# The second layer's output projection: its last quarter of rows multiplied in plain fp32 instead of as three rounded products

## The chip, the core and the metric

The kernel runs on one core of a Trainium2 chip. The metric is the device time of one execution in microseconds (us). The engines are TensorE (PE, with its weight loads listed apart as PEld), VectorE (DVE), ScalarE (ACT), GpSimd (POOL) and SyncE (SP); here SP only issues the transfers from device memory, in order, and an issue waits on its queue until the buffer it writes is free.

## What is computed

A two-layer decoder trunk over 256 positions of width 2048, all in fp32. The change concerns the last line of the second layer's token mixer, `o @ w_o`, a product of 256x2048 by 2048x2048.

```python
def swa_attention(h, pos, w_in, sinks, w_o):      # layer 1: window 128, 32 heads of 64
    ...
    o = jnp.einsum('bnhgqk,bnkhd->bnqhgd', p, vb).reshape(B, S, Hq * dh)
    return o @ w_o

for i in range(DEPTH):                            # DEPTH = 2
    ...
    h = x * (1.0 + sc1) + sh1
    y = fox_attention(...) if i == 0 else swa_attention(...)
    x = layer_norm(DEEPNORM_ALPHA * x + (1.0 + g1) * y, ...)
    h = x * (1.0 + sc2) + sh2
    y = conv_ffn(h, ...)
    x = layer_norm(DEEPNORM_ALPHA * x + (1.0 + g2) * y, ...)
```

## The kernel before

**Three products for one.** Weights arrive as fp32. `stream` loads them in tiles `w` of 128 partitions x 4 row blocks x 512 columns (1 MB), six buffers in rotation (pool `wp`, shared with the tiles `wa` of the conditioning matrix and `ln` of the norm rows). Two row blocks at a time are split: ACT copies them to `wh` in fp32r, a rounded format that TensorE takes in one go (L255), and DVE puts the rest, `w - wh`, into `wl` (L259). `wh` and `wl` have four buffers each. The other operand is split in the same way, and TensorE adds the products high x high, high x low and low x high in PSUM (`x_mm`).

**Whole products.** A row block `kc` that `stream` finds in `whole` isn't split: it calls `add(kc, w, None, use)`, and `x_mm` then issues one fp32 product of `w` as loaded with an unsplit stationary tile. Before the change layer 0 does this for kc 4-7 and 12-15, layer 1 for none. `o_tile` decides the same for the attention's result `o`: an unsplit one is one ACT copy into a tile `oW` (L784); a split one is an ACT cast (L84) and a DVE subtraction (L85) into `oT`, or, for kc 12-15, into the free rows of the large tile `hH`.

```python
        if kc in WHOLE[l]:
            ...
            nc.scalar.copy(o, src)
            return o, None
...
                if l is None:
                    mm(ps[t], xh, h[:, i, :], start=kc + i == first, stop=kc + i == last)
                    continue
                mm(ps[t], xh, h[:, i, :], start=kc + i == first)
                mm(ps[t], xh, l[:, i, :])
                mm(ps[t], xl, h[:, i, :], stop=kc + i == last)
```

**The projection's course.** `out_proj` makes four column blocks d = 0 to 3 of 512, each for two blocks t = 0, 1 of 128 positions, over 16 row blocks kc: 128 products by 128x512, each threefold in layer 1. Row block kc is the result of two heads. For d = 0 and 1 the kc run in the order 0-7, 8-11, 12-15, between the attention of the last heads (scores `S`, softmax `pr`, transposes `T` and their copies `pT`, results `o`), since `stat` steps the attention on until the result it needs is there. d = 2 and d = 3 follow without attention between.

**The edge.** In the last block, d = 3, `x_mm_end` does kc 8-15 for t = 0 first and then for t = 1. While t = 1 runs, `Edge.end` has DVE finish t = 0: residual (L658, L660), statistics (L662, L665), scaling (L688); then TensorE transposes `x` (`sm`, L539) and ACT and DVE make the next input `hH` (L548 to L552) for the first block of the following ConvFFN, `head_block`. For this block of d = 3 the splits of kc 8 to 15 go to spare places, so that they can be made ahead: kc 8, 10 and 12 into unused room of `hH`, kc 14 into small tiles `eh` and `el`.

**Order.** The instructions of an engine run in a fixed order, chosen by the tile scheduler at build time; buffers that come free decide when a waiting transfer starts.

Of the kernel before, what the change touches and what calls it, by code (L numbers as in the profile page):

```python
# [21 lines left out]
KC = D // P  # L22
# [19 lines left out]
def hybrid_trunk(ctx: ExitStack, tc: tile.TileContext, a: dict, out: bass.AP):  # L42
# [186 lines left out]
    def stream(wsrc, row0, col, ks, use, spare={}, whole=()):  # L229

        ks, pend = list(ks), {}
        for kc in ks[::2]:
            g = row0 + kc
            src = wsrc[g // UK, col // WB]
            if kc in pend:
                w = pend[kc]
            elif g % UK == 0 and kc + 2 in ks:
                W = wtile()
                pin(nc.sync.dma_start(W, src), False)
                w, pend[kc + 2] = W[:, :2], W[:, 2:]  # L240
            else:
                if halves:
                    w = halves.pop()
                else:
                    W = wtile()
                    w = W[:, :2]
                    halves.append(W[:, 2:])
                pin(nc.sync.dma_start(w, src[:, g % UK:g % UK + 2]), False)
            if kc in whole:
                add(kc, w, None, use)  # L250
                continue
            h, l = spare[kc]() if kc in spare else (hl.tile([P, 2, WB], F32R, tag=n, name=n) for n in ("wh", "wl"))
            pieces = [(h, l, w)] if not isinstance(h, Pair) else [(h[:, i, :], l[:, i, :], w[:, i, :]) for i in range(2)]
            for hp, _, wp_ in pieces:
                pin(nc.scalar.copy(hp, wp_), False)  # L255

            def split_(pieces=pieces):
                for hp, lp, wp_ in pieces:
                    nc.vector.tensor_tensor(lp, wp_, f32(hp), op=ALU.subtract)  # L259

            add(kc, h, l, use, split_)
# [22 lines left out]
    def x_mm(ps, kc, h, l, stat, last, first=0, ts=range(NT), js=range(2)):  # L284

        for t in ts:
            for i in js:
                xh, xl = stat(kc + i, t)
# [7 lines that stand above are left out]
    def x_mm_end(ps, stat, nk, n, edge=None):  # L296

        kept = []

        def use(kc, h, l):  # L300
            end = kc >= nk - 2 * n
            x_mm(ps, kc, h, l, stat, nk - 1, ts=(0,) if end else range(NT))
            if end:
                kept.append((kc, h, l))
            if kc + 2 >= nk:
                for i, e in enumerate(kept):
                    if edge:
                        edge(i, ps)
                    x_mm(ps, *e, stat, nk - 1, ts=(1,))
                if edge:  # L310
                    edge(n, ps)

        return use
# [46 lines left out]
    def spares(nk, n, held=False):  # L360
        at = lambda o: hpad[:, o:o + 2 * WB].rearrange("p (a f) -> p a f", a=2)
        if n == 8:
            return {nk - 16 + 2 * i: lambda i=i: (at(32 + i * 4 * WB), at(32 + (2 * i + 1) * 2 * WB)) for i in range(4)}
        out = {nk - 8 + 2 * i: lambda i=i: (at(32 + i * 2 * WB), at(60 + (8 + 2 * i) * WB)) for i in range(4)}
        if held:
            out[nk - 2] = lambda: (Pair("eh"), Pair("el"))
        return out
# [402 lines left out]

    AV = ((0, 0, 2 * P), (P, 2 * P, 3 * P))

    WHOLE = ((*range(4, 8), *range(12, KC)), ())

    wide = []

    def o_tile(kc, src, l):

        if kc in WHOLE[l]:
            if not wide:  # L780
# [13 lines left out]
    def out_proj(oT, full, w_o, l, edge):  # L794
# [7 lines left out]
        def part(d, ks):  # L802
            if d == D // WB - 1:
                stream(w_o, 0, d * WB, ks, x_mm_end(ps[d], stat, KC, HEAD, edge.end), spares(KC, HEAD, True), WHOLE[l])
            else:
                stream(w_o, 0, d * WB, ks, lambda kc, h, l_: x_mm(ps[d], kc, h, l_, stat, KC - 1), whole=WHOLE[l])

# [487 lines left out]
```

## Time and profile before

| | |
|---|---|
| median of 3 runs | 2180.22 us (2179.78 to 2181.76) |
| the profiled execution | 2180.01 us, of which 2178.1 us are the span from the first to the last instruction |
| granted TensorE clock | 0.997 |
| busy | PE 98%, PEld 88%, DVE 80%, ACT 53%, POOL 1% |
| transfers | 598.60 MB, 275 GB/s in the mean |
| layer 1's output projection, kc 12-15 and the edge | about 1380 to 1455 us of the span |

In the rows shown below, a timeline row is the start in us, the duration in us from the first start to the last end, engine, line, operation, output<-inputs, shape and how many instructions are merged in it; in brackets stands idle time of the engine just before it and what ended it. In a row of a group, after the bar, stand busy us and mean ns of one, then idle us before such instructions and what ended it. Matmuls overlap in the pipeline, so the rate of a stretch is read from start to start and not from the durations. The chain is the work that ended last, followed back from the end. Line 75 is the helper that issues every product; a product is told by its tiles.

### The profile page before, as it was taken

The page shows a single profiled execution, that of the slowest core. Times are in us where ns is not written, and L with a number is a line of the kernel's source. Part 1 is how long each engine was busy: PE and PEld are TensorE (multiplying, and loading weights), DVE is VectorE, ACT ScalarE, POOL GpSimd, SP SyncE. Part 2 cuts the span into 40 slices and gives each one's busy share as a digit, 9 for nine tenths or more (in the row PEclk, how much of TensorE's full clock was granted, in tenths as well). Part 3 has the DMA queues.
Part 4 walks back from the last instruction along what each step waited for, and adds up shares of the span by engine and source line. Part 5 has one row for each costly group of instructions (what it writes and reads, how often), then busy time and mean ns, then how long its engine had stood idle before and what let it go on. Part 6 is the DMA issues. An engine that isn't in the chain of part 4 may idle for free.

```text
span 2178.1 us, 35629 instructions
## 1 busy us (share of the span) xinstructions
PE 2133.7 (98%) x14424; PEld 1916.9 (88%) x14424; DVE 1742.4 (80%) x2400; ACT 1151.8 (53%) x1788; POOL 11.8 (1%) x34
## 2 busy tenths in 40 slices
PE   6999999999999999999999999999999999999997
PEld 6999887579999888999987877779999888999986
DVE  7988898779989988988997897679788655666765
ACT  4546565255575433555555577555555633555541
POOL 1000000000000000000000000000000000000000
PEclk9999999999999999999999999999999999999999
DMA  9998988949888989887885665547777555555552
GB/s 389 420 370 305 372 333 333 370 173 352 312 298 316 341 346 356 328 325 291 327 332 224 239 251 195 183 144 299 271 271 272 198 194 195 194 194 194 192 195 100
DMA packets 89654, 598.60 MB, mean 275 GB/s; under 512 B 10016, under 2 KB 12352, under 8 KB 21136
## 3 DMA queue, kind: packets, MB, share of 16 engines
q1 hardware_dynamic: 89312, 595.87, 73.9%
q8 instruction: 113, 1.85, 0.3%
q0 software_dynamic: 176, 0.44, 0.1%
q14 instruction: 53, 0.43, 0.0%
HBM read 594.18 MB, written 2.10 MB: 274 GB/s over the span
## 4 chain that ended last, share of the span: by engine, by line
PE 84%; DVE 9%; ACT 4%; DMA 2%; issue 1%; SPq 0%; POOL 0%; DVEq 0%; ACTq 0%; POOLq 0%
PE ws L75 46%; PE xs L75 35%; DVE wa L420 3%; DVE wl L259 2%; DMA w<-in_fox_w_in_dram 2%; ACT wh L255 1%; DVE pr L735 1%; PE o L75 1%; PE S L75 1%; ACT pr L739 0%; PE T L766 0%; ACT hH L551 0%; PE sm L75 0%; PE sm L502 0%; DVE hH L552 0%
## 5 line engine op out<-in xcount | busy, mean ns | idle before, releaser
L255 ACT CAST wh<-w 128x1024 fp32r<-128x1024 f32 x698 | 733.0, 1053 | 726.8 <-PE ws L75 340.2
L259 DVE TENSOR_TENSOR wl<-w,wh 128x1024 fp32r<-128x1024 f32 x698 | 847.8, 1221 | 328.6 <-ACT wh L255 326.1
L75 PE MATMUL ws<-hH,wh 128*128 128x256 f32 x6400 | 1098.0, 276 | 8.3 <-ACT hH L529 7.5
L75 PEld LDWEIGHTS ws<-hH,wh 128*128 128x128 f32 x6400 | 968.3, 188 | 11.7 <-ACT hH L529 7.9
L75 PE MATMUL ws<-hH,wl 128*128 128x256 f32 x3200 | 879.9, 276 | 2.4 <-DVE wl L259 2.4
L75 PEld LDWEIGHTS ws<-hH,wl 128*128 128x128 f32 x3200 | 601.2, 188 | 3.4 <-DVE wl L259 3.3
L420 DVE CUSTOM_DVE_ANT_0 wa<-wa,cb,acol 128x2048 f32<-128x2048 f32 x192 | 449.4, 2344 | 2.1 <-DMA wa<-in_ada_w_dram 1.9
L75 PE MATMUL xs<-wh,gT 128*128 128x512 f32 x1344 | 414.7, 389 | 0.0
L75 PEld LDWEIGHTS xs<-wh,gT 128*128 128x128 f32 x1344 | 252.3, 188 | 52.1
L75 PE MATMUL xs<-wl,gT 128*128 128x512 f32 x672 | 261.4, 389 | 0.0
L75 PE MATMUL xs<-wh,hH 128*128 128x512 f32 x752 | 254.0, 403 | 6.5 <-ACT wh L255 3.2
L75 PEld LDWEIGHTS xs<-wh,hH 128*128 128x128 f32 x752 | 140.3, 189 | 40.3 <-ACT wh L255 3.7
L75 PE MATMUL xs<-wl,hH 128*128 128x512 f32 x376 | 148.9, 396 | 2.5 <-DVE wl L259 2.5
L75 PEld LDWEIGHTS xs<-wl,gT 128*128 128x128 f32 x672 | 126.1, 188 | 26.3
L1150 ACT ACTIVATE u<-ws,ccol 128x256 f32<-128x256 f32 x176 | 96.7, 561 | 52.3 <-PE ws L75 42.1
L75 PE MATMUL xs<-wh,oT 128*128 128x512 f32 x288 | 96.1, 401 | 1.1 <-ACT wh L255 1.1
L1151 DVE SCALAR_TENSOR_TENSOR u<-ws,ccol,u 128x255 f32<-128x255 f32 x176 | 82.1, 476 | 14.4 <-ACT u L1150 14.4
L75 PEld LDWEIGHTS xs<-wl,hH 128*128 128x128 f32 x376 | 71.0, 189 | 16.9 <-DVE wl L259 3.2
L1153 DVE SCALAR_TENSOR_TENSOR u<-ws,ccol,u 128x254 f32<-128x254 f32 x176 | 83.1, 476 | 2.2
L75 PEld LDWEIGHTS xs<-wh,oT 128*128 128x128 f32 x288 | 53.9, 188 | 13.2 <-ACT wh L255 1.3
L739 ACT ACTIVATE pr<-pr,nm 128x128 f32<-128x128 f32 x96 | 43.2, 452 | 32.0 <-DVE nm L735 31.9
L658 DVE TENSOR_TENSOR t<-xs,gate 128x512 f32<-128x512 f32 x48 | 31.5, 683 | 35.0 <-PE xs L75 35.0
(213 smaller groups left out, 1268.6 us busy)
## 6 DMA issues: line engine op xcount, KB each, us to landing
wa<-in_ada_w_dram SPq DMA_DIRECT2D x192, 1024.0 KB, 6.7
w<-in_ffn_w_up_dram SPq DMA_DIRECT2D x176, 1024.0 KB, 5.3
w<-in_ffn_w_down_dram SPq DMA_DIRECT2D x88, 1024.0 KB, 5.0
w<-in_fox_w_in_dram SPq DMA_DIRECT2D x60, 512.0 KB, 8.7
w<-in_swa_w_in_dram SPq DMA_DIRECT2D x20, 1024.0 KB, 5.7
w<-in_fox_w_in_dram SPq DMA_DIRECT2D x18, 1024.0 KB, 7.5
w<-in_fox_w_o_dram SPq DMA_DIRECT2D x16, 1024.0 KB, 7.3
w<-in_swa_w_o_dram SPq DMA_DIRECT2D x16, 1024.0 KB, 4.8
```

The costliest lines, as they stand in the source:

```text
L75: return nc.tensor.matmul(o, lhsT, rhs, start=start, stop=stop, **kw)
L255: pin(nc.scalar.copy(hp, wp_), False)
L259: nc.vector.tensor_tensor(lp, wp_, f32(hp), op=ALU.subtract)
L420: return nc.vector.tensor_tensor_reduce(w, w, cb, 1.0, acol[:, l, v * KC + k:v * KC + k + 1], ALU.mult, ALU.add, cv[:, k:k + 1])
L658: pin(nc.vector.tensor_tensor(tmp, ps[t], gate[:, d * 512:(d + 1) * 512], op=ALU.mult), end)
L735: nc.vector.tensor_tensor_reduce(pr[:, b:e].rearrange("p (a k) -> p a k", k=P), S_ps[:, b:e].rearrange("p (a k) -> p a k", k=P), mk, -1.0, ...
L739: nc.scalar.activation(pr[:, b:e], pr[:, b:e], AF.Exp, bias=nm[:, r:r + 1], scale=-1.0, accum_out=ss[:, r:r + 1])
L1150: nc.scalar.activation(u, pf, AF.Identity, bias=cw(CW, f), scale=cw(2, f))
L1151: nc.vector.scalar_tensor_tensor(u[:, 1:], pf[:, :S - 1], cw(1, f), u[:, 1:], op0=ALU.mult, op1=ALU.add)
L1153: nc.vector.scalar_tensor_tensor(u[:, 2:], pf[:, :S - 2], cw(0, f), u[:, 2:], op0=ALU.mult, op1=ALU.add)
```

## The change

In layer 1 the row blocks kc 12-15 are no longer split: neither the weights (for all four d) nor the attention's results.

```diff
-    WHOLE = ((*range(4, 8), *range(12, KC)), ())
+    WHOLE = ((*range(4, 8), *range(12, KC)), range(12, KC))
```

32 products (4 kc x 4 d x 2 t) of three instructions become 32 of one. Eight splits of weights go (six of the `wh`/`wl` pairs, one in `hH`, one in `eh`/`el`), and four splits of `o` become copies. It also moves instructions. On TensorE, at the last heads' attention, the stretch of kc 12-15 began so before, in d = 0 (`T` transposes softmax rows, `o` is an attention result, and the `hH` here holds the split `o` of kc 12-15):

```order
L766 MATMUL T<-ident,pr 128x128 x3
L75 MATMUL xs<-wh,hH 128x512
L75 MATMUL xs<-wl,hH 128x512
...
L75 MATMUL xs<-wh,hH 128x512
L75 MATMUL o<-pT,V 64x256 x2
L75 MATMUL o<-pT,V 64x128 x2
L766 MATMUL T<-ident,pr 128x128 x6
L75 MATMUL xs<-wh,hH 128x512
L75 MATMUL xs<-wl,hH 128x512
L75 MATMUL o<-pT,V 64x256 x2
L75 MATMUL o<-pT,V 64x128 x2
```

And begins so now, on the same engine at the same place, to the end of d = 1:

```order
L766 MATMUL T<-ident,pr 128x128 x3
L75 MATMUL xs<-w,oW 128x512 x4
L75 MATMUL o<-pT,V 64x256 x2
L75 MATMUL o<-pT,V 64x128 x2
L766 MATMUL T<-ident,pr 128x128 x4
L75 MATMUL xs<-w,oW 128x512
L766 MATMUL T<-ident,pr 128x128 x2
L75 MATMUL o<-pT,V 64x256
L75 MATMUL xs<-w,oW 128x512
L75 MATMUL o<-pT,V 64x256
L75 MATMUL o<-pT,V 64x128 x2
L75 MATMUL xs<-w,oW 128x512 x10
```

The attention's steps keep their order, and the whole products stand between them singly: one splits the six transposes, one the last `o`.

On TensorE at the edge (d = 3, the end of t = 1, with the transposes `sm` of the new `x`), the difference from before (-) to now (+):

```order
-L75 MATMUL xs<-hH 128x512 x3
+L75 MATMUL xs<-w,oW 128x512
 L539 MATMUL sm<-ident,x 128x128 x4
-L75 MATMUL xs<-hH 128x512 x3
+L75 MATMUL xs<-w,oW 128x512
 L539 MATMUL sm<-ident,x 128x128 x4
-L75 MATMUL xs<-eh,hH 128x512
-L75 MATMUL xs<-el,hH 128x512
-L75 MATMUL xs<-eh,hH 128x512 x2
-L75 MATMUL xs<-el,hH 128x512
-L75 MATMUL xs<-eh,hH 128x512
+L75 MATMUL xs<-w,oW 128x512 x2
```

The transposes stay where they were; one whole product stands ahead of them, one between the two groups and two behind, where three, three and six rounded ones were.

On SP's queue the transfers keep their order, and what they wait for changes. The last two tiles of this projection's weights and the first of the next ones stood so before (a `DMAHW` wait is for an earlier transfer, the other one for the engine that frees the buffer):

```order
L239 DMA w<-in_swa_w_o_dram 128x2048 [waits DMAHW1_49,DVE_49]
L239 DMA w<-in_swa_w_o_dram 128x2048 [waits DMAHW2_49,DVE_49]
L239 DMA w<-in_ffn_w_up_dram 128x2048 [waits DMAHW3_49,DVE_49]
...
L239 DMA w<-in_ffn_w_up_dram 128x2048 [waits DMAHW5_49,DVE_49]
L239 DMA w<-in_ffn_w_up_dram 128x2048 [waits DMAHW6_49,DVE_49]
L239 DMA w<-in_ffn_w_up_dram 128x2048 [waits DMAHW1_49,DVE_49]
L239 DMA w<-in_ffn_w_up_dram 128x2048 [waits DMAHW2_49,DVE_49]
```

And so now:

```order
L239 DMA w<-in_swa_w_o_dram 128x2048 [waits DMAHW7_49,PE_49]
L239 DMA w<-in_swa_w_o_dram 128x2048 [waits DMAHW0_49,PE_49]
L239 DMA w<-in_ffn_w_up_dram 128x2048 [waits DMAHW7_49,DVE_49]
...
L239 DMA w<-in_ffn_w_up_dram 128x2048 [waits PE_49]
L239 DMA w<-in_ffn_w_up_dram 128x2048 [waits DMAHW1_49,DVE_49]
L239 DMA w<-in_ffn_w_up_dram 128x2048 [waits DMAHW2_49,DVE_49]
L239 DMA w<-in_ffn_w_up_dram 128x2048 [waits DMAHW0_49,PE_49]
```

A tile read as loaded is freed by TensorE's last product with it, no longer by DVE's subtraction: the four transfers that wait for PE are those that take such a tile's buffer. On ACT the casts of d = 3's kc 8 and 10 now stand ahead of the last ten of the `wh`.

## Prediction

> **What bounds the kernel now.** I read first the busy times and the chain of the page, then TensorE's waits around the place of the change, 1340 to 1480 us.
>
> ```profile
> span 2178.1 us, 35629 instructions
> PE 2133.7 (98%) x14424; PEld 1916.9 (88%) x14424; DVE 1742.4 (80%) x2400; ACT 1151.8 (53%) x1788; POOL 11.8 (1%) x34
> PE 84%; DVE 9%; ACT 4%; DMA 2%; issue 1%; SPq 0%; POOL 0%; DVEq 0%; ACTq 0%; POOLq 0%
> PE S L75 <- DVE qL L85: 0.8, 1, 0.8
> PE xs L75 <- ACT hH L84: 0.7, 1, 0.7
> PE sm L539 <- DVE x L688: 0.6, 1, 0.6
> ```
>
> TensorE is busy 98% of the span and holds 84% of the chain. In these 140 us it waits three times, 2.1 us in all, and never for a split of weights. So time is made or lost here by the TensorE time of the products, except at the edge, where 0.6 and 0.7 us say that DVE and ACT end last. The splits themselves are early, as the ACT and DVE groups of 1352 to 1440 us show:
>
> ```profile
> L255 ACT CAST wh<-w 128x1024 fp32r<-128x1024 f32 x24 | 25.2, 1048 | 21.0 <-PE xs L75 20.7
> L84 ACT CAST hH<-o 128x256 fp32r<-128x256 f32 x4 | 1.5, 368 | 1.0 <-PE o L75 1.0
> L259 DVE TENSOR_TENSOR wl<-w,wh 128x1024 fp32r<-128x1024 f32 x25 | 30.5, 1222 | 20.7 <-ACT wh L255 20.6
> L85 DVE TENSOR_TENSOR hH<-o,hH 128x256 fp32r<-128x256 f32 x4 | 1.7, 419 | 0.9 <-ACT hH L84 0.9
> ```
>
> ACT sat idle 20.7 us before its casts until TensorE gave a `wh` back: it waits for TensorE, not the other way round.
>
> **What is removed costs nothing and brings nothing.** Off ACT go eight casts of 1.05 us, 8.4 in all. Off DVE go eight subtractions of 1.22 and four of 0.42: 11.4 us. (One cast and one subtraction of the eight are made in halves, for `eh` and `el`; I price them as whole.) All this lay beside TensorE's stream. The four copies of `o` stay at about 0.37 us. What could be won by it is at most the 1.3 us of waits at the edge; since there DVE and ACT run the norm and no split of this projection, I take 0 and keep -1.3 as the lower end.
>
> **The price of a product.** Layer 0 has the same whole products, with the same shapes.
>
> ```profile
> L75 PE MATMUL xs<-w,oW 128*128 128x512 f32 x128 | 57.0, 593 | 0.0
> 377.52 3.60 PE L75 MATMUL xs<-w,oW 128*128 128x512 f32 x8
> 380.96 0.82 PE L75 MATMUL o<-pT,v 128*128 128x256 f32 x4
> 406.96 7.03 PE L75 MATMUL xs<-w,oW 128*128 128x512 f32 x16
> 1394.74 0.39 PE L75 MATMUL xs<-wh,oT 128*128 128x512 f32 x1
> 1411.06 0.39 PE L75 MATMUL xs<-wh,hH 128*128 128x512 f32 x1
> 1416.50 0.39 PE L75 MATMUL xs<-wh,oT 128*128 128x512 f32 x1
> ```
>
> Layer 0 makes 8 kc x 4 d x 2 t = 64 such products, and the first row counts 128: each leaves two records. Sixteen records from 406.96 take 7.03 to the last one's end; less its own 0.59 that is 6.44 over 15 starts, 0.429 each, and the eight from 377.52 to 380.96 give 0.430. A whole product takes 0.859 us. The rounded ones: d = 2 runs 96 of them from 1394.74 to 1416.50, 0.2267 each, 0.680 for three. A whole product costs 0.179 us more than the three it replaces, and all 32 would cost 5.7 us if nothing hid any of it.
>
> The Trainium skill, TensorE: Matmul & The Clock Gate, section Back-to-back issue gap, gives about 131 ns for a 512-column matmul in a stream with weight loads, and about 216 ns from its formula for an isolated gap. With the four passes that the Trainium skill, FP8 and Floating Point Precision, section TensorE Precision Notes, gives for true fp32, an estimate from these pages is that a product would cost 0.13 us more by the first and 0.22 by the second, 4.2 or 6.9 us over 32. The 0.2267 here agrees with neither, and the rows decide.
>
> **d = 2.** 24 rounded products from 1411.06 to 1416.50, 5.44 us, become 8 whole ones, 6.87: +1.43 on the path.
>
> **d = 0 and 1, among the attention.**
>
> ```profile
> 1380.60 0.49 PE L766 MATMUL T<-ident,pr 128*128 128x128 f32 x3
> 1380.85 0.49 PE L75 MATMUL xs<-wh,hH 128*128 128x512 f32 x1
> 1383.80 0.87 PE L75 MATMUL o<-pT,V 128*64 128x256 f32 x8
> 1384.60 0.88 PE L766 MATMUL T<-ident,pr 128*128 128x128 f32 x6
> 1385.28 0.50 PE L75 MATMUL xs<-wh,hH 128*128 128x512 f32 x1
> 1385.93 1.04 PE L75 MATMUL o<-pT,V 128*64 128x256 f32 x8
> 1386.90 0.73 PE L75 MATMUL xs<-wh,hH 128*128 128x512 f32 x2
> ```
>
> From 1380.60 to 1394.74 pass 14.14 us. `T` and `o` take 0.25, 0.80, 0.68 and 0.97 of it, start to next start; 11.44 are left for 48 rounded products, 0.56 more than 48 x 0.2267, lost at the switches to and from `T` and `o`. Sixteen whole ones take 13.74: +2.30 if these switch losses vanish, as in layer 0, where the eight records ahead of `o` at 380.96 ran at full rate; +2.86 if they stay. New is that two groups are cut up: one whole product follows the first four of the transposes and needs the new copy of `o`, and the last `o` is split around another. The copy, 0.37 us, has the four transposes as cover (about 0.45, two thirds of the 0.68 above); the copies `pT` have whole products of 0.86. I take 0.15 for what isn't covered, so +2.45, between 2.30 and 2.86.
>
> **d = 3 and the edge.**
>
> ```profile
> 1430.15 1.55 PE L75 MATMUL xs<-hH 128*128 128x512 f32 x6
> 1432.92 2.94 PE L75 MATMUL xs<-hH,oT 128*128 128x512 f32 x12
> 1433.12 0.69 DVE L658 TENSOR_TENSOR t<-xs,gate 128x512 f32<-128x512 f32 x1 [3.23 <-PE xs L75]
> 1437.11 0.65 PE L539 MATMUL sm<-ident,x 128*128 128x128 f32 x4 [0.57 <-DVE x L688]
> 1437.52 0.93 PE L75 MATMUL xs<-hH 128*128 128x512 f32 x3
> 1438.29 0.60 PE L539 MATMUL sm<-ident,x 128*128 128x128 f32 x4
> 1438.64 0.48 PE L75 MATMUL xs<-eh,hH 128*128 128x512 f32 x1
> 1440.12 0.39 PE L75 MATMUL xs<-wh,hH 128*128 128x512 f32 x1
> 1440.64 0.68 DVE L658 TENSOR_TENSOR t<-xs,gate 128x512 f32<-128x512 f32 x1
> 1443.17 0.42 DVE L552 TENSOR_TENSOR hH<-t,hH 128x256 fp32r<-128x256 f32 x1
> 1443.64 0.73 PE L75 MATMUL xs<-wh,hH 128*128 128x512 f32 x2
> 1454.58 0.50 PE L75 MATMUL xs<-wh,hH 128*128 128x512 f32 x1 [0.73 <-ACT hH L84]
> ```
>
> For t = 0, the twelve from 1430.15 to 1432.92, 2.77 us, become four whole, 3.44: +0.67 on the path, since DVE starts the norm when they end. For t = 1, four whole ones replace twelve too, but here a cover exists. The transposes at 1437.11 wait for DVE, 4.19 us after t = 0's end; ahead of them one whole product replaces three rounded ones, +0.18, inside the 0.57 of waiting. Behind them three whole ones (2.58) replace the nine of 1437.52 to 1438.29 and 1438.64 to 1440.12 (2.25): t = 1 ends 0.33 later. DVE needs that end for its residual at 1440.64, and as it took 0.20 from 1432.92 to 1433.12, it could have begun at 1440.32; with 0.33 more it begins at 1440.65. DVE stays the later one, by a hair. The next block's products would then reach the place of 1443.64, where they awaited DVE's row of 1443.17, about 0.1 late. I take +0.10, with 0.72 as the upper end (nothing hidden) and 0 as the lower. If this cover goes, the residual of t = 1 is what starts late, and with it the wait shown at 1454.58.
>
> **The transfers.** Four issues on SP wait for TensorE now, and those behind them in its queue wait too.
>
> ```profile
> w<-in_swa_w_o_dram SPq DMA_DIRECT2D x16, 1024.0 KB, 4.8
> 1392.36 0.33 SPq L239 DMA_DIRECT2D w<-in_swa_w_o_dram  x1
> 1429.91 0.33 SPq L239 DMA_DIRECT2D w<-in_ffn_w_up_dram  x1
> 1464.41 1.06 ACT L255 CAST wh<-w 128x1024 fp32r<-128x1024 f32 x1 [1.75 <-PE xs L75]
> ```
>
> The tile with d = 3's kc 8-11, issued at 1392.36, now waits for d = 0's last whole product, about 1391 (1380.60, nine whole products, 2.70 of `T` and `o`), so it lands with the 4.8 of the first row near 1396. Its two casts now stand ahead of those for d = 2's kc 8 on ACT. With two casts of 1.05 before, one for itself and a subtraction of 1.22, that split would be ready near 1400.5; it is needed 48 rounded products, 10.9 us, after d = 2's start near 1397: cover of some 7 us. The last of the four, issued at 1429.91 before, waits for the edge's end near 1445, and its tile is cast at about 1464 + 5: cover some 19 us for a 5 us transfer. Both 0; the price of a miss is in the rivals.
>
> **The sum.** 2.45 + 1.43 + 0.67 + 0.10 = 4.65. On the profiled execution's 2180.01 us (2178.1 of span and 1.9 around it), which stands 0.21 below the median 2180.22, that is 2184.7, a little past the 0.2% (4.4 us, about what a measurement of this kernel tells from no change).
>
> **Rivals.** *Nothing of the edge is hidden, and the switch losses stay*: 2.86 + 1.43 + 0.67 + 0.72 = 5.7, so 2185.7. For it speaks how thin the cover is (0.01 us by the row of 1440.64), against it the 0.57 us of waiting.
>
> *Less than 0.2%*: no switch is lost, t = 1 is hidden whole, and the lighter ACT and DVE shorten the edge's waits by up to 1.3: 2.30 + 1.43 + 0.67 - 1.3 = 3.1, so 2183.1. For it speaks that the edge is DVE's and ACT's; against it, that after 1433 us neither has a split that is removed.
>
> *Faster, the other side*: a whole product costs one record. Its place is each of the 32, its price 0.429 against 0.680, -8.0 us, so 2172.0; it decides if a product issues below 0.680. For it stands that each record, 0.429, is below that; against it the count of 128 for 64 products and the eight records between 377.52 and 380.96, which are one `w` pair's four products (two kc, two t). The Trainium skill, Perfetto Trace Analysis, section Engine Utilization, halves the array's rate for FP32_LOW_HIGH; were that a whole product's rate, it would be this rival, and the trace has 0.859 against 0.2267, about a quarter of the rate.
>
> *A late tile*: d = 2's kc 8 casts starve behind those of `hH`. If the tile landed a whole landing time (4.8) past the cover of 7, TensorE would wait about 5 more: 2189.5. Nothing in the queue's rows speaks for a delay of 12 us.
>
> **Chances.** Forecast 0.58, nothing hidden 0.20, less than 0.2% 0.15, faster 0.03, late tile 0.04. The forecast lies at the threshold, so about half of its 0.58 falls on either side: slower 0.30 + 0.20 + 0.04 = 0.54, same 0.28 + 0.15 = 0.43, faster 0.03. The range reaches over the first two rivals, 2183.1 to 2185.7, with 0.1 below and 0.5 above, since of the shown runs (2179.78 to 2181.76) the median lies nearer the fast end: 2183.0 to 2186.2. Left out are faster, late tile and a tenth of the rest.
>
> **What would show it.** In the trace after: 64 more `w,oW` records at 0.43 from start to start; d = 2 about 1.4 longer than 21.76; 1380.60 to d = 2's start about 16.6 instead of 14.14; the wait for `x` near 0.4 instead of 0.57; from t = 0's end to the place of 1454.58 the same 21.7 us within 0.2. Wrong would it be made by a wait of TensorE at d = 2's kc 8, by a longer edge, or by whole products that run at another rate beside the 64-column `o`.

## The result, and the profile after

The changed kernel takes 2187.36 us, median of 7 runs (2185.91 to 2188.41); the kernel before, run beside it, 2180.07 (2179.41 to 2181.76). The ratio is 1.0032 with a 95% interval of 1.0023 to 1.0041: slower by 7.3 us, where the prediction had 4.65, and outside its range of 2183.0 to 2186.2. The profiled execution of the changed kernel is the one at 2187.36, with a granted clock of 0.997 as before.

The head of its page, the chain by engine, and TensorE's waits from 1340 to 1480 us, as shown of before:

```profile
span 2185.4 us, 35534 instructions
PE 2139.9 (98%) x14392; PEld 1911.2 (87%) x14392; DVE 1732.9 (79%) x2387; ACT 1144.2 (52%) x1779; POOL 11.8 (1%) x34
PE 84%; DVE 9%; ACT 4%; issue 1%; DMA 1%; SPq 0%; POOL 0%; DVEq 0%; ACTq 0%; POOLq 0%
PE S L75 <- DVE qL L85: 0.8, 1, 0.8
PE xs L75 <- ACT hH L84: 0.7, 1, 0.7
PE sm L539 <- DVE x L688: 0.4, 1, 0.4
```

TensorE is busy 6.2 us longer (2139.9 against 2133.7), DVE 9.5 and ACT 7.6 us less (the prediction had 11.4 and 8.4), and the waits around the change are the three of before, 1.9 us in all instead of 2.1. The view lists no new wait (it leaves out those under 0.15 us): the time went into TensorE's own work. The groups of the changed kernel by line and tiles:

```profile
L75 PE MATMUL xs<-w,oW 128*128 128x512 f32 x192 | 86.2, 594 | 0.0
L259 DVE TENSOR_TENSOR wl<-w,wh 128x1024 fp32r<-128x1024 f32 x692 | 840.9, 1221 | 332.2 <-ACT wh L255 329.8
L255 ACT CAST wh<-w 128x1024 fp32r<-128x1024 f32 x692 | 726.6, 1053 | 730.2 <-PE ws L75 339.7
```

The 64 more records of whole products are there, 192 instead of 128, and six `wh`/`wl` pairs fewer.

To see where the 7.3 us lie, the run is cut at four places that both traces have: the last copy `qb` of layer 1's queries (before the change takes effect), the three transposes `T` ahead of kc 12-15, the first `wl,oT` product of d = 2 and of d = 3, and the edge, the product that waits for `hH`. TensorE's rows of the changed kernel from `T` to d = 2, those of rounded products left out:

```profile
1380.88 0.49 PE L766 MATMUL T<-ident,pr 128*128 128x128 f32 x3
1381.21 3.60 PE L75 MATMUL xs<-w,oW 128*128 128x512 f32 x8
1384.74 0.87 PE L75 MATMUL o<-pT,V 128*64 128x256 f32 x8
1385.54 0.66 PE L766 MATMUL T<-ident,pr 128*128 128x128 f32 x4
1386.08 1.12 PE L75 MATMUL xs<-w,oW 128*128 128x512 f32 x2
1387.04 0.38 PE L766 MATMUL T<-ident,pr 128*128 128x128 f32 x2
1387.35 0.65 PE L75 MATMUL o<-pT,V 128*64 128x256 f32 x2
1387.93 1.12 PE L75 MATMUL xs<-w,oW 128*128 128x512 f32 x2
1388.98 0.86 PE L75 MATMUL o<-pT,V 128*64 128x256 f32 x6
1389.78 8.85 PE L75 MATMUL xs<-w,oW 128*128 128x512 f32 x20
1398.70 0.39 PE L75 MATMUL xs<-wl,oT 128*128 128x512 f32 x1
```

and its later landmarks, TensorE's first `wl,oT` of d = 3 and the edge, with DVE's two residuals:

```profile
1421.93 0.40 PE L75 MATMUL xs<-wl,oT 128*128 128x512 f32 x1
1439.00 0.69 DVE L658 TENSOR_TENSOR t<-xs,gate 128x512 f32<-128x512 f32 x1 [3.90 <-PE xs L75]
1446.70 0.69 DVE L658 TENSOR_TENSOR t<-xs,gate 128x512 f32<-128x512 f32 x1 [0.38 <-PE xs L75]
1460.66 0.50 PE L75 MATMUL xs<-wh,hH 128*128 128x512 f32 x1 [0.73 <-ACT hH L84]
```

The same two `wl,oT` rows of the kernel before:

```profile
1394.96 0.39 PE L75 MATMUL xs<-wl,oT 128*128 128x512 f32 x1
1416.72 0.39 PE L75 MATMUL xs<-wl,oT 128*128 128x512 f32 x1
```

`wl,oT`, the second product, is taken because a first rounded product that follows a whole one has a longer record (0.79 instead of 0.39), so its start isn't comparable. The times between landmarks:

| stretch | before | after | longer by | predicted |
|---|---|---|---|---|
| start to `qb` | 1332.06 | 1332.32 | 0.26 | 0 |
| `qb` to `T` | 48.54 | 48.56 | 0.02 | 0 |
| d = 0 and 1 (`T` to d = 2) | 14.36 | 17.82 | 3.46 | 2.45 |
| d = 2 | 21.76 | 23.23 | 1.47 | 1.43 |
| d = 3 to the edge | 37.86 | 38.73 | 0.87 | 0.77 |
| edge to the last row of `x` | 718.44 | 718.45 | 0.01 | 0 |
| last row of `x` to the end | 5.08 | 6.33 | 1.25 | 0 |

The last row of `x` is the start of the last row of L1250 in DVE's timeline (two instructions in one row), 2173.02 and 2179.11 us. So there are two surprises: 1.0 us in d = 0 and 1, and 1.2 us after the last computation, 720 us away from the change. The 0.26 at the start precedes every changed instruction; other executions have `qb` between 1332.3 and 1334.2, so it is the scatter of a run.

The edge of the kernel before holds 0.28 us that the prediction didn't see. ACT's second cast of the new `hH` waits 0.79 us for DVE there; in the changed kernel, and in three kernels further down whose layer 1 is that of before, it waits 0.51. The row of the kernel before, then that of one of the three (kc 4-7 whole in layer 0):

```profile
1439.85 0.41 ACT L551 CAST hH<-t 128x256 fp32r<-128x256 f32 x1 [0.79 <-DVE t L550]
```

```profile
1436.72 0.41 ACT L551 CAST hH<-t 128x256 fp32r<-128x256 f32 x1 [0.51 <-DVE t L550]
```

The cast starts 0.36 us after DVE has released it, where the other starts after 0.08. DVE's rows behind it, the residual at 1440.64 among them, are later by the same 0.28 us. The ACT instructions that come 128 and 256 places later in its stream, waits counted (1536.43 and 1650.84), start 0.28 us late as well, against the same instructions of the kernel with kc 4-7; and 0.65 us behind the first two of the three a packet of q14, an instruction queue, starts. So it looks like a refill of ACT's instructions that falls on the edge in the kernel before and elsewhere in the others; no run tests this by itself. The three kernels take 37.58 us from d = 3 to the edge, not 37.86: against them the change costs 1.15 us there instead of 0.87.

The end of both kernels, the before one first: SP's wait for the last output transfer, and the transfer itself in the 4 us from 1.4 us after the last `x` row (queues, then the issue with its time to landing):

```profile
SPq L1291 <- DMA out_dram<-x: 2.0, 1, 2.0
q1 hardware_dynamic: 288, 0.52, 34.4%
out_dram<-x SPq DMA_DIRECT2D x1, 256.0 KB, 2.3
```

```profile
SPq L1291 <- DMA out_dram<-x: 3.3, 1, 3.3
q1 hardware_dynamic: 288, 0.52, 34.8%
q14 instruction: 1, 0.01, 0.5%
out_dram<-x SPq DMA_DIRECT2D x1, 256.0 KB, 3.6
```

The last output transfer lands 1.3 us later after its issue, and in the same 4 us one packet of an instruction queue, q14, has run.

### The profile page after: what moved, and what is told of

Read it like the earlier page. It is cut to its first block, busy times and chain, and to the rows that moved or that the text cites. A ratio compares the mean times of both kernels' runs of the same rounds, so it can differ in the third digit from the quotient of the medians.

```text
span 2185.4 us, 35534 instructions
## 1 busy us (share of the span) xinstructions
PE 2139.9 (98%) x14392; PEld 1911.2 (87%) x14392; DVE 1732.9 (79%) x2387; ACT 1144.2 (52%) x1779; POOL 11.8 (1%) x34
## 4 chain that ended last, share of the span: by engine, by line
PE 84%; DVE 9%; ACT 4%; issue 1%; DMA 1%; SPq 0%; POOL 0%; DVEq 0%; ACTq 0%; POOLq 0%
PE ws L75 46%; PE xs L75 36%; DVE wa L420 3%; DVE wl L259 3%; ACT wh L255 1%; DMA w<-in_fox_w_in_dram 1%; PE o L75 1%; DVE pr L735 1%; ACT pr L739 0%; PE T L766 0%; PE S L75 0%; PE sm L75 0%; PE sm L502 0%; ACT dl L457 0%; ACT hH L551 0%
## 5 line engine op out<-in xcount | busy, mean ns | idle before, releaser
L75 PE MATMUL xs<-wh,hH 128*128 128x512 f32 x704 | 238.8, 404 | 5.6 <-ACT wh L255 2.3
L75 PEld LDWEIGHTS xs<-wh,hH 128*128 128x128 f32 x704 | 131.4, 189 | 37.3 <-ACT hH L84 3.5
L75 PE MATMUL xs<-wl,hH 128*128 128x512 f32 x352 | 139.5, 396 | 3.3 <-DVE wl L259 3.3
L75 PE MATMUL xs<-w,oW 128*128 128x512 f32 x192 | 86.2, 594 | 0.0
L75 PEld LDWEIGHTS xs<-wl,hH 128*128 128x128 f32 x352 | 66.6, 189 | 17.0 <-DVE wl L259 4.0
L75 PEld LDWEIGHTS xs<-w,oW 128*128 128x128 f32 x192 | 35.4, 190 | 37.2 <-issue 35.5
```

Source lines behind the costliest of these rows:

```text
L75: return nc.tensor.matmul(o, lhsT, rhs, start=start, stop=stop, **kw)
```

## The experiments

All times and ratios are against runs of the kernel before on the same chip. "Stretch" is from `qb` to the edge, 122.52 us before and 128.34 after (+5.82); the 0.28 us at the edge stand in the kernel before alone, so against the three kernels without them every such difference is 0.3 larger.

**Cutting or count?** Theory A: the 1.0 us in d = 0 and 1 comes from whole products that cut the groups `T` and `o` into pieces. Rival B: a whole product simply costs more here than in layer 0, so the cost goes by the number of products. In the first kernel both row blocks of a pair are awaited before the first of its whole products, so `T` and the last `o` stay together; everything else is the changed kernel.

```diff
-                stream(w_o, 0, d * WB, ks, lambda kc, h, l_: x_mm(ps[d], kc, h, l_, stat, KC - 1), whole=WHOLE[l])
+                def use(kc, h, l_):
+                    if l == 1 and l_ is None:
+                        stat(kc, 0), stat(kc + 1, 0)
+                    x_mm(ps[d], kc, h, l_, stat, KC - 1)
+
+                stream(w_o, 0, d * WB, ks, use, whole=WHOLE[l])
```

> The change, with one thing more: both row blocks of a pair are awaited before its first whole product is written, so that on TensorE no whole product cuts a group of transposes or of attention results (after the last pair's six transposes one whole product, then all of o, then eleven whole ones). Theory A (the cutting made kc 12-15 of d = 0 and 1 dearer than forecast): the stretch from the last three transposes ahead of these products to d = 2, 14.14 us before and 17.59 with the change, falls to about 16.7, and the time lies about 0.9 us below the change's, 4.9 above before. Theory B (whole products among attention are dearer by themselves, about 0.22 instead of 0.15 us each): the stretch stays at 17.6 and the time with it.

Measured: 2185.29 us, median of 8 runs (2184.85 to 2188.15), ratio 1.0024 [1.0014, 1.0034]; the stretch is 127.37, +4.85, so 0.97 less than in the changed kernel. (The median, 2.1 us below the changed kernel's, says less: the runs of either scatter by 2.5 us or more.) TensorE's rows of this kernel at the same place:

```profile
1382.71 0.49 PE L766 MATMUL T<-ident,pr 128*128 128x128 f32 x3
1383.03 3.60 PE L75 MATMUL xs<-w,oW 128*128 128x512 f32 x8
1386.56 0.87 PE L75 MATMUL o<-pT,V 128*64 128x256 f32 x8
1387.36 0.88 PE L766 MATMUL T<-ident,pr 128*128 128x128 f32 x6
1388.07 1.02 PE L75 MATMUL xs<-w,oW 128*128 128x512 f32 x2
1389.03 0.87 PE L75 MATMUL o<-pT,V 128*64 128x256 f32 x8
1389.83 9.71 PE L75 MATMUL xs<-w,oW 128*128 128x512 f32 x22
1399.60 0.39 PE L75 MATMUL xs<-wl,oT 128*128 128x512 f32 x1
```

From `T` to d = 2 it is 16.89 us, 2.53 more than before and 0.93 less than in the changed kernel. For an order without cuts the prediction had 2.30 (its 2.45 holds 0.15 for the cuts), so 0.23 of the switch losses stay. The rows show where the 0.93 are. From the first of the six transposes to the first `o`, with one whole product between, the changed kernel takes 1.81 us (1385.54 to 1387.35) and this one 1.67 (1387.36 to 1389.03): the cut of `T` costs 0.14. From that `o` to the long run of whole products it is 2.43 with one whole product inside (1387.35 to 1389.78), and here 0.80 with none (1389.03 to 1389.83), or 1.66 with a whole product's 0.86 added: the cut of `o` costs 0.77.

The trace shows why a cut-off `o` is dear. The products of the two heads of a row block are written to the two halves of one tile by turns, and uncut they run two at a time: in this kernel the eight records start in four pairs, 7 ns apart within a pair, and the first two pairs 0.27 us apart. The single product that the changed kernel puts ahead of the whole one (two records at 1387.35) has lost its partner, and its two records start 0.27 us apart all the same. So alone it holds TensorE 0.58 us, where all eight records take 0.80, and the six left over still take 0.80. The whole product between the pieces takes 1.05 instead of 0.86. The cut of `T` is in part a wait too short for the view: the whole product behind the four transposes starts 0.06 us after ACT's copy of `o` ends (1385.65 + 0.37).

The second kernel keeps the number of whole products and moves them to kc 8-11, where the attention's groups aren't cut.

```diff
-    WHOLE = ((*range(4, 8), *range(12, KC)), range(12, KC))
+    WHOLE = ((*range(4, 8), *range(12, KC)), range(8, 12))
```

> Whole products in layer 1 for kc 8-11 instead of 12-15: the same 32 products, also among the attention for d = 0 and 1 (in fours between groups of three transposes, none cut), at the edge ahead of the transposes. Theory A (cutting): 4 x 0.6 = 2.4 us for d = 0 and 1, 1.4 for d = 2, 0.7 for t = 0 of d = 3, 0.1 for t = 1 (0.57 us of waiting takes the rest): 4.6 above before, about 2184.7. Theory B (dearer among attention by themselves): 3.4 + 1.4 + 0.7 + 0.1 = 5.6 above before, about 2185.7.

Measured: 2186.43 us (2185.68 to 2187.68, 8 runs), 1.0027 [1.0017, 1.0037]; the stretch is 127.17, +4.65, where theory A had 4.6 and B 5.6. The sum is nearer A, but its parts aren't A's: +1.89 to the start of d = 2 (A 2.4), +1.44 in d = 2 (1.4) and +1.33 from there to the edge (0.8). The evidence for the cuts is the kernel before this one and the two that follow.

Two kernels with half of the whole products, kc 14 and 15 (nothing is cut) and kc 12 and 13 (`T` and `o` are cut, by one whole product and by rounded ones):

```diff
-    WHOLE = ((*range(4, 8), *range(12, KC)), range(12, KC))
+    WHOLE = ((*range(4, 8), *range(12, KC)), (14, 15))
```

> The changed kernel with only kc 14 and 15 whole in layer 1 (16 products instead of 32); kc 12 and 13 are rounded and multiplied three times, as before. The first row block of a pair now has no whole product, so the transposes T stay together, as in the run with both row blocks awaited. Theory A (a whole product costs 0.18 more than three rounded ones, and cutting T and o costs the 0.9 to 1.0 beside it): half of that run's 4.85 us over before, 2.2 to 2.5 us from the query bias to the edge. Rival B (the whole cost goes by the number of products): half of the changed kernel's 5.82 us, 2.9. For the end: with 5 to 8 more instructions on VectorE than in the changed kernel the q14 transfer comes some 3 to 5 us earlier, so the wait for the output is 2.0 us.

> The changed kernel with only kc 12 and 13 whole in layer 1 (16 products). Here the first row block of a pair brings whole products and the second rounded ones, and T and o are cut up as in the changed kernel, but with one whole product and rounded ones in the cuts. If a cut costs the same whatever stands in it, the stretch from the query bias to the edge is 2.4 + 0.9 = 3.3 us longer than before; if only whole products in a cut cost, it lies between, at 2.4 to 3.0; rival B (by the number of products) gives 2.9. For the end, as with kc 14 and 15: a wait of 2.0 us.

Measured, one execution each: the stretch is +2.42 for kc 14 and 15 (A: 2.2 to 2.5, B: 2.9; with the 0.3 of the edge it would lie between) and +3.04 for kc 12 and 13, which by itself would fit B too. The landmarks decide: `T` to d = 2 takes +1.27 with kc 14 and 15, half of the 2.53 without cuts and not half of the 3.46 with them, and +2.12 with kc 12 and 13; d = 2 takes +0.73 in both, and d = 3 to the edge +0.39 and +0.20. So the cuts cost 0.85 with rounded products in them, nearly the 0.93 that they cost with whole ones, and 0.77 of it is again the cut of `o` (1388.58 to 1390.38 in its trace, less 0.23 for the rounded product inside and the 0.80 of an uncut group). The sum missed the expected 3.3 mostly at the edge, where kc 12 and 13, which come earlier in d = 3, cost less.

**Do the terms add?** Whole products in d = 0 and 1 alone, the others rounded (the core of the edit, with `PARTS = (0, 1)`):

```diff
-                stream(w_o, 0, d * WB, ks, lambda kc, h, l_: x_mm(ps[d], kc, h, l_, stat, KC - 1), whole=WHOLE[l])
+                on = l == 0 or d in PARTS
+                st = stat_w if on else stat
+                stream(w_o, 0, d * WB, ks, lambda kc, h, l_: x_mm(ps[d], kc, h, l_, st, KC - 1), whole=WHOLE[l] if on else ())
```

> The changed kernel with whole products in layer 1 only for the column blocks d = 0 and 1; for d = 2 and 3 the same rows are rounded and multiplied three times, and the attention output is both copied and split. If the terms simply add, the stretch from the query bias to the edge is 3.45 us longer than before, and d = 2, the products of t = 0 and the edge take what they took before. If instead the longer start is given back or carried on at the edge, it differs from 3.45 by more than 0.3.

Measured, one execution: +2.34, not 3.45, and that is a miss of mine: in this kernel the six transposes and the eight `o` stand together again (its `T` row reads x6), probably because `o` is both split and copied. So it is one more kernel without cuts, and `T` to d = 2 takes +2.54, the 2.53 of the first experiment. d = 2 takes what it took before (+0.02). From d = 3 to the edge it takes 37.60 us, 0.26 less than before and the 37.58 of the three kernels with an unaltered layer 1. So the terms add, with 2.53 for the order without cuts.

**The end.** The changed kernel again, unaltered, tells chance from property:

> The change again, unaltered. If the 1.2 us that its profile shows after the last output transfer is issued (the end waits 3.3 us for it, 2.0 before) belongs to the change, the profile shows 3.3 again and the median lies 7.0 to 7.4 above before. If it is chance, the end waits anything from 2.0 to 3.3 and the median lies 5.8 to 6.6 above before, 5.8 being what the two traces differ by from the first changed product to the end of the edge.

Measured: 2187.28 us (2185.5 to 2188.2, 9 runs), 1.0028 [1.0018, 1.0038]; the stretch +5.82, the end 6.27, its wait 3.2. The 1.2 us come again, and they came in the two kernels above with all 32 products too (waits of 3.1 and 3.2). In each of these four traces one q14 packet starts 3.1 to 3.7 us after the last row of `x`, while the last output is under way; in the kernel before, the last one is 13 us ahead of that row. Theory: the instruction stream of DVE or ACT has become shorter, so that one of its refills falls on the last output. Rival: something else of the change. DVE lost 13 instructions and ACT 9, so these were put back as dummies at the program's start, on one engine at a time:

```diff
+    pad = cst.tile([1, 2], F32, name="pad")
+    for _ in range(13):
+        nc.vector.memset(pad, 0.0)
```

```diff
+    pad = cst.tile([1, 2], F32, name="pad")
+    nc.gpsimd.memset(pad, 0.0)
+    for _ in range(9):
+        nc.scalar.copy(pad[:, 1:2], pad[:, 0:1])
```

> The changed kernel with 13 tiny memsets (1 x 2 elements) added on VectorE ahead of its first work, as many instructions as the change took from VectorE (2400 before, 2387 after). Theory A: the last output transfer takes 1.2 us longer in the changed kernel because a transfer of the instruction queue q14 starts at the same time, and it does so because VectorE's instruction stream is shorter; with the 13 put back no q14 transfer stands in the last 3 us, the end's wait for the output is 2.0 instead of 3.3 us, the time from the last row of x to the end 5.1 instead of 6.2 to 6.3, and the stretch from the query bias to the edge stays 128.3. Rival B: the end belongs to something else of the change (or q14 there to another engine): the wait stays 3.1 to 3.3 us.

> The changed kernel with 9 copies of one element added on ScalarE ahead of its work, as many instructions as the change took from ScalarE (1788 before, 1779 after), and one memset on GpSimd. If the q14 transfer at the end is ScalarE's, the end's wait for the output is 2.0 us here and stays 3.2 with VectorE's padding; if it is VectorE's, it is the other way round; if it is neither's, both stay at 3.1 to 3.3.

Measured, one execution each: with DVE's 13 the time is 2186.25, the end 5.1 and its wait 2.0; with ACT's 9 it is 2188.79, 6.6 and 3.4. The stretch is +5.79 and +5.75, unchanged. SP's wait, the queue and the last transfer of the kernel with DVE's dummies:

```profile
SPq L1294 <- DMA out_dram<-x: 2.0, 1, 2.0
q1 hardware_dynamic: 288, 0.52, 34.5%
out_dram<-x SPq DMA_DIRECT2D x1, 256.0 KB, 2.4
```

No q14 packet runs there any more; the last is 12.7 us ahead of the last row of `x`. So the refill is DVE's, and its place is a matter of DVE's instruction count: with 2400 instructions (before, and these dummies), 2396, 2394 and 2393 (the kernels with d = 0 and 1, kc 12, kc 14), and with the 2412 to 2425 of the three kernels below, the wait is 2.0; with 2387 or 2388 it is 3.1 to 3.4. The Trainium skill, Runtime: NRT & Kernel Launch, section Instruction fetch mechanics, says that each engine's sequencer fetches its own next block through its own DMA queue while it runs, at a cost that is mostly hidden. The traces agree that a block comes while the engines run. In the profile's list, however, q14 holds the refills of more than one engine: ACT's nine dummies move others of its packets, one from 152.5 to 163.1 us ahead of the last row of `x`, and leave this one. And here is a refill that isn't hidden: beside the last output, where nothing follows to cover it, it goes with 1.2 us.

How one packet of 0.01 MB does it can be seen in the changed kernel's last packets, from 2182.61 to 2182.86 and from 2182.86 to 2183.11 us:

```profile
q14 instruction: 1, 0.01, 7.7%
```

```profile
q1 hardware_dynamic: 1, 0.00, 0.2%
```

The output (q1) moves its bytes in about the same time after its issue as before, and ends with packets of 4 bytes. All of these but one have started by 2182.20; the last starts at 2183.10, as the q14 packet ends (2182.79, 0.31 us long), and the landing waits for it. The other four traces with the long end have the same order, in two of them with one data packet between. So the output's last packet stands behind the refill.

**Do whole products pay at all?** Layer 0 has had them all along. The kernel before without any, in either layer:

```diff
-    WHOLE = ((*range(4, 8), *range(12, KC)), ())
+    WHOLE = ((), ())
```

> No whole products at all, in layer 0 neither (layer 1 as before the change). Theory C (whole products pay only where DVE is short): TensorE does 64 x 0.179 = 11.5 us less, but DVE gets 16 subtractions of 1.22 and 8 of 0.42 more, 22.9 us, in a stretch of 124 us where it was busy for 96.4, so DVE becomes the bound and at most 4.7 us are won, at the worst some 5 lost: 2175 to 2185. Rival (TensorE is the bound there too): 11.5 us less than before, 2168.7.

Measured: 2184.96 us (2183.44 to 2186.01, 11 runs), 1.002 [1.0011, 1.0029], the upper end of what was expected. `qb` comes at 1338.40, 6.3 us later than before, and the stretch in layer 1 is that of before within 0.3 us. So whole products save time in layer 0 and cost time in layer 1. Half of them in layer 0, none in layer 1, the last quarter or the second one:

```diff
-    WHOLE = ((*range(4, 8), *range(12, KC)), ())
+    WHOLE = (range(12, KC), ())
```

```diff
-    WHOLE = ((*range(4, 8), *range(12, KC)), ())
+    WHOLE = (range(4, 8), ())
```

> The kernel before with half of its whole products: in layer 0's output projection only the last quarter of the rows (kc 12 to 15) is multiplied whole, kc 4 to 7 are rounded and multiplied three times; layer 1 has no whole products, as before. Theory C: in layer 0 TensorE is full from 350 to 444 us (94.0 of 94 busy) and VectorE has 26.6 us free there, so half of the whole products takes some 4.7 us from TensorE (half of the 9.4 that no whole product at all took from its busy time there) and gives VectorE 9.6, which fits: the query bias of layer 1 comes 4 to 5 us earlier and the time is 2175 to 2177 us. Rival D: VectorE is already full at 320 to 350 us (28.98 of 30 busy) and the added rounding falls there, so the delay goes by the count: half of the 6.3 us that the kernel without whole products loses, some 2183 us.

> The same with the other half: in layer 0 only kc 4 to 7 are multiplied whole, kc 12 to 15 are rounded; layer 1 has none. Theory C gives the same 2175 to 2177 us. Rival D: some 2183 us. If the two halves differ by more than 2 us, it is not the amount of VectorE's work that counts but where in a pair of row blocks it stands: rounding kc 12 to 15 comes last in each column block and would be late for it, so this one would be the slower.

Measured: with kc 12-15 whole 2185.63 us (2183.22 to 2186.97, 11 runs), 1.0021 [1.0012, 1.0030]; with kc 4-7 whole 2177.26 (2176.52 to 2178.61, 11 runs), 0.9987 [0.9978, 0.9996]. This one beats both kernels: 3.2 us faster than before and 10.1 than the changed one. That the halves would differ by more than 2 us if the place counts was right; which of them is slower I had the wrong way round. TensorE's waits for the second part of the weights, from 340 to 460 us, in the kernel before, without whole products, with kc 12-15 and with kc 4-7 whole, one fence each:

```profile
PE xs L75 <- DVE wl L259: 0.5, 1, 0.5
```

```profile
PE xs L75 <- DVE wl L259: 9.9, 5, 4.3
```

```profile
PE xs L75 <- DVE wl L259: 7.2, 3, 4.3
```

```profile
PE xs L75 <- DVE wl L259: 2.0, 2, 1.4
```

and the stretch from 410 to 444 us of the same four, in the same order (busy us and number of PE, PEld, DVE, ACT and POOL, the granted clock, the DMA share, GB/s):

```profile
410.00:444.00 34.00, 34.00 (x109) 20.32 (x108) 22.34 (x25) 8.00 (x8) 0.00 (x0) 1.00 0.95 376
```

```profile
410.00:444.00 34.00, 25.14 (x91) 19.23 (x91) 30.02 (x35) 12.26 (x13) 0.00 (x0) 0.85 0.85 317
```

```profile
410.00:444.00 34.00, 27.56 (x91) 19.36 (x92) 26.51 (x30) 9.95 (x10) 0.00 (x0) 0.90 0.85 329
```

```profile
410.00:444.00 34.00, 32.55 (x126) 23.18 (x125) 28.85 (x35) 10.39 (x12) 0.00 (x0) 1.00 0.97 376
```

In layer 0 DVE can be the late one. Each half gives TensorE back 32 products at 0.179, 5.7 us. Without whole products TensorE waits 9.9 us for DVE, with kc 12-15 whole 7.2, with kc 4-7 whole only 2.0; and where it waits long, its granted clock falls too, to 0.85 and 0.90 of full in these 34 us, where the other two keep 1.00. For kc 4-7 theory C's time was right within 0.3 us, but `qb` comes only 2.8 us earlier than before, not 4 to 5. For kc 12-15 it was wrong, and rival D's 2183 was too low as well. Both halves give DVE nearly the same amount of work (2412 and 2413 instructions, 1752.4 and 1752.6 us busy), so the amount doesn't decide; what goes with the loss is that TensorE waits for it. The waits and the clock don't account for the whole 6.3 and 3.7 us by which `qb` is later in the two slow ones; the rest was not followed.

## Why the prediction was right and where it was wrong

- **The bound** was right. TensorE's own time decided; no wait was removed that mattered, and the 9.5 us off DVE and 7.6 off ACT brought nothing from 1340 us on. After the edge nothing was given back: 718.45 us against 718.44.
- **The price of a whole product**, 0.859 us against 0.680, was right: d = 2 took +1.47 (predicted 1.43), and with kc 14 and 15 alone +0.73.
- **d = 0 and 1** is the first term that failed: +3.46 measured, +2.45 predicted, upper bound 2.86. The step that failed is the price of the two cuts, 0.15 "for what isn't covered". I had seen both cuts in the order and priced them as a copy that must arrive in time. For the cut of `T` that was right, 0.14, and in part for that reason. The cut of `o` I put at nothing, and it cost 0.77, as TensorE time: a product cut off from its partner runs alone. Together they cost 0.93 (17.82 against 16.89), 0.85 in the pair of kernels with half the products. The other 0.23 are switch losses that I let vanish as in layer 0; without cuts the term was 2.53, not 2.30. The bound of 2.86 kept the switch losses of before, but the new order has more switches.
- **d = 3 and the edge**: +0.87 for 0.77, and that closeness is luck. t = 0 was right (+0.67 from the start of d = 3 to DVE's first residual, 17.07 against 16.40). For t = 1 I took 0.10, since DVE's residual at 1440.64 left a cover "by a hair". That row held the 0.28 us of ACT's late cast, which the change moves away. In the changed kernel DVE waits there 0.38 us for TensorE, so the cover was gone. From t = 0's residual to the edge it is 21.66 us (1439.00 to 1460.66) against 21.46 in the kernel before, within the 0.2 that I allowed, but 21.19 in the three kernels with an unaltered layer 1: +0.47 for my 0.10. The wait for `x` fell from 0.57 to 0.39, as foretold (about 0.4).
- **The transfers** were right in their effect. The late tile of d = 3's weights was there for its casts at 1397.46, 1.5 us after the forecast, and TensorE waited neither for it nor for the casts behind it:

```profile
1397.46 1.99 ACT L255 CAST hH<-w 128x1024 fp32r<-128x1024 f32 x2 [7.20 <-DMA w<-in_swa_w_o_dram]
1401.43 1.06 ACT L255 CAST wh<-w 128x1024 fp32r<-128x1024 f32 x1 [1.98 <-PE xs L75]
```

- **The end** was in no step and in no rival, so it was put at nothing: +1.25 us in the profiled execution. I counted instructions that were removed only by their time, not by what their number does to the stream they are fetched in. The page had the instruction queues in its list, and the last output transfer at the chain's end.

Between the medians lie 7.29 us, 2.64 more than the 4.65. The end gives 1.25 of it, the cut of `o` 0.77, the switch losses 0.23, the edge 0.10 (0.38 for the lost cover, less 0.28 for the late cast that went) and d = 2 0.04; the other 0.25 is about what the profiled run loses at its start, 0.26. The rivals fared no better: "nothing of the edge is hidden, and the switch losses stay" came nearest (2185.7) for reasons that hold in part, 0.47 of its 0.72 and 0.23 of its 0.56.

## What to carry to other kernels

When a longer instruction takes the place of short ones among interleaved work, price the order it makes: count how many groups are cut, look in the trace whether their members run side by side, and what a short group costs against a long one, before asking whether its data arrive in time. An edit that trades one engine's time for another's has to be read stage by stage: the same edit paid where VectorE was late (layer 0, kc 4-7) and cost where TensorE was never kept waiting (layer 1). And before a difference of a microsecond at the very end is put down to the change, look whether an instruction fetch has moved onto the last transfer; a handful of dummy instructions tells.

## What the runs showed of the hardware that I had not expected

- The `o` products of two heads, 64 columns each, run side by side: their starts are 7 ns apart. A product cut off from its partner takes as long as the pair: one alone (two records) holds TensorE 0.58 us between other shapes, three 0.80 and four 0.80, start to next start.
- One packet of DVE's instruction fetch beside the last output goes with 1.2 us at the end, since the output's last packet starts only as the fetch ends. Its place moves in jumps with DVE's instruction count: it stood 12.6 to 12.9 us ahead of the last row of `x` with 2393 to 2400 instructions and 3.1 to 3.7 us behind it with 2387 and 2388.
- In the kernel before, three ACT instructions 128 places apart start 0.28 us late, the first two of them 0.65 us ahead of a q14 packet. One stands on the edge, and the change, which takes instructions off ACT, moves it away.
